# Thirteen more tiles of a two-block transformer are transposed on VectorE in 32 by 32 blocks

## Chip, core and metric

One core of a Trainium2 chip runs the whole program. The metric is the device time of one execution in microseconds, and of several executions the median. A profile is one further execution, recorded by the hardware profiler.

## What is computed

The reference takes 256 tokens of width 2048 through two transformer blocks, in float32. The first block has three mixers side by side (gated linear attention GLA, forgetting attention FoX, attention over a memory), a gated output projection and a feed-forward network. The second has an NSA attention with compressed, selected and window keys, a pooling mixer, a cross attention and a gated feed-forward network. Cut to what matters here:

```python
xn = rms_norm(h, attn_norm_g)
proj = xn @ w_in                      # gq gk gv gg ga fq fk fv fg ff mq mg
gla_o = gla_chunked(gq, gk, gv, log_a)
fq_h, fk_h = rms_norm(fq, fox_q_norm_g), rms_norm(fk, fox_k_norm_g)
fox_o = forgetting_attention(fq_h, fk_h, fv, log_f)
mk = rms_norm(mk, mem_k_norm_g); mq_h = rms_norm(mq, mem_q_norm_g)
mem_o = softmax(mq_h @ mk.T * 128 ** -0.5) @ mv
o = rms_norm(concat(gla_o, fox_o, mem_o), out_norm_g)
h = h + (o * gate) @ w_out
u = relu(rms_norm(h, mlp_norm_g) @ w_up)
h = h + (u * u) @ w_down
# second block: z = rms_norm(h, ...) @ w_in_2, a = nsa_attention(...), ... a @ w_br_attn
```

## The kernel before

**Weights and groups.** Each product with a weight matrix is a list of groups, one for each 512 output columns. A group has two PSUM banks, one for each half of 128 tokens, and takes 16 k-tiles of 128 rows. The product is made in three passes of fp32r numbers: a matrix is split into a high part (`wh`, a copy on ScalarE, line 133) and a low part (`wl`, a subtraction on VectorE, line 367), and so is the stationary operand (H and L). For each k-tile and each half there are three matmuls, H wh (line 461), H wl (462) and L wh (463). So a group is 96 matmuls of 512 columns. A unit is two k-tiles, 512 KB of weights, split in one instruction on each of the two engines. There are five raw buffers, filled from SyncE's queue, and six pairs wh, wl; a unit is split about four units ahead of its use (`AHEAD`).

**Order.** All engines' orders are written by a planner while the program is built. It walks through the groups in a fixed list (mk mv, then gq gk sm gv0 gv1 mq fq fk fv gg0 gg1 fg mg, out0 to out3, the feed-forward groups, then those of block 2). After every k-tile it calls `pump`, which first emits due weight splits and then lets tasks take a step each, as long as ScalarE and VectorE are by its own costs no more than `LIM` = 3500 ns behind TensorE. Tasks are generators: what is done with a finished group (its eviction, norms, transposes) and the attentions. A task that starts when another one has set an event (`until`) goes by the instruction having been emitted.

**Transposes.** H must have the model dimension on its partitions, so a result of 256 tokens by 512 columns, a tile of 128 x 1024 numbers, is transposed. `T_group` does it on TensorE: eight transposes of 128 x 128 (line 203) in two groups of four, each group into one of four PSUM banks `pb`, from which ScalarE and VectorE take the result, with a gain or split into H and L (`T_split`, `T_plain`). `T_dve` does it on VectorE, into another SBUF tile: 16 instructions of 32 partitions x 256 numbers (line 526), each of which transposes eight blocks of 32 x 32 and puts them in their places through its access pattern; then ScalarE copies H and VectorE subtracts to L. Before the change `T_dve` serves the tiles u of the first feed-forward network and those of the second, 27 in all.

**Who reads the tiles.** mkT, mqT, fqT and fkT are read by the score matmuls of memory attention and FoX (small matmuls, line 197); gqT and gkT by multiplications on VectorE in GLA, which feed small matmuls; the gated outputs by out0 to out3, four k-tiles each in the order of the tiles; the normed tiles h by up0 and all later up groups, in the same way; the two NSA outputs by four groups late in block 2.

Of the kernel before, what the change touches and what calls it, by code (L numbers as in the profile page):

```python
# [10 lines left out]
F32 = mybir.dt.float32  # L11
# [3 lines left out]
OP = mybir.AluOpType  # L15
# [93 lines left out]
class Program:  # L109
# [406 lines left out]

        yield from self.T_group(nat, sink)

    def T_dve(self, f, hi, lo):

        (g,) = yield from self.F.wait()
        x = f.rearrange("p (t k q j) -> p k t q j", t=2, k=4, q=4)
        y = g.rearrange("p (k t a i) -> p k t a i", k=4, t=2, a=4)
        for a in range(4):
            for q in range(4):
                self.nc.vector.transpose(y[32 * q:32 * q + 32, :, :, a], x[32 * a:32 * a + 32, :, :, q])  # L526
                self.dv(256)
                if q % 2:
                    yield 1
        self.F.put(f)  # L530
        self.act(hi, g)
        yield 1
        self.tt(lo, g, hi.bitcast(F32), OP.subtract)
        self.F.put(g)

    def T_plain(self, nat, dst, gain=None):
# [69 lines left out]
def v3(f, a):  # L606
    return f.rearrange("p (a b) -> p a b", a=a)


class Kernel(Program):  # L610
# [57 lines left out]
    def headnorm_T(self, banks, key, gain, name):  # L668
        yield from self.until(("rs", key))
        rs = self.rs[key]  # L670
        f, j = yield from self.F.wait(2)
        for t in range(2):
            self.scopy(v3(f, 2)[:, t], banks[t], rs[:, t:t + 1])
        yield "B"
        self.act(j, f, AF.Square)
        yield 1
        ss = self.stat(8)
        self.red(ss, v3(j, 8), OP.add)
        self.F.put(j)
        r = self.rstd(ss, 8, 128.0)  # L680
        yield 1
        self.tt(v3(f, 8), v3(f, 8), r[:, :, None].to_broadcast([128, 8, 128]), OP.mult)
        yield 1
        (o,) = yield from self.F.wait()
        yield from self.T_plain(v3(f, 2), o, gain)
        self.F.put(f)
        self.S[name] = o
        self.ev.add(name)

    def plain_T(self, banks, key, scale, name, keep=False):  # L690
        yield from self.until(("rs", key))
        rs = self.rs[key]
        if scale != 1.0:
            r2 = self.stat(2)
            self.ts(r2, rs, scale)
            rs = r2
        f, o = yield from self.F.wait(2)
        for t in range(2):
            self.scopy(v3(f, 2)[:, t], banks[t], rs[:, t:t + 1])
        yield "B"  # L700
        yield from self.T_plain(v3(f, 2), o)
        if keep:
            self.S["nat", name] = f
        else:
            self.F.put(f)
        self.S[name] = o
        self.ev.add(name)
# [316 lines left out]
    def gate(self, banks, grp, silu):  # L1024
        rs = self.rs["x"]
        (s,) = yield from self.F.wait()
        s3 = v3(s, 2)
        for t in range(2):
            self.act(s3[:, t], banks[t], AF.Sigmoid, scale=rs[:, t:t + 1])
            if silu:  # L1030
                self.stt(s3[:, t], banks[t], rs[:, t:t + 1], s3[:, t], OP.mult, OP.mult)
        if grp == 3:
            self.free_TT("x")
        yield "B"
        yield from self.until(("o", grp))
        o = self.S.pop(("o", grp))
        self.tt(o, o, s, OP.mult)
        self.F.put(s)
        yield 1
        h, l = yield from self.R.wait(2)  # L1040
        yield from self.T_split(v3(o, 2), self.vec("out_norm_g", 4 * grp, 4), h, l)
        self.F.put(o)
        self.TT["o"][0][grp], self.TT["o"][1][grp] = h, l
        self.ev.add(("oT", grp))

# [4 lines left out]
    def norm_T(self, f, c, key, gain, sq):  # L1050

        f3 = v3(f, 2)
        self.sq_into(f3, sq, c)
        self.nsq[key] = self.nsq.get(key, 0) + 1
        if self.nsq[key] == 4:
            self.fin_ssq(sq, key)
        yield 1
        h, l = yield from self.R.wait(2)
        yield from self.T_split(f3, self.vec(gain, 4 * c, 4), h, l)
        H, L = self.TT.setdefault(key, ([None] * 4, [None] * 4))  # L1060
        H[c], L[c] = h, l
        self.ev.add((key, c))
# [392 lines left out]

    def a_T(self, f, x):
        h, l = yield from self.R.wait(2)
        yield from self.T_split(v3(f, 2), None, h, l)
        self.F.put(f)
        self.TT["a"][0].append(h)  # L1460
        self.TT["a"][1].append(l)
        self.ev.add(("a", x))
# [697 lines left out]
```

## Time and profile before

| | us |
|---|---|
| median of 3 runs | 2615.86 (2615.46 to 2617.05) |
| the profiled execution, own time | 2612.74 |
| its span, first to last instruction | 2611.0 |
| TensorE busy | 2589.7 |
| VectorE busy | 1671.8 |
| ScalarE busy | 1265.4 |

TensorE was granted its full clock for 0.998 of the span. Matmuls are pipelined: the next one begins before the last one's record ends, so busy times of several lines of TensorE add up to more than the span, and the pace is read from the distance of starts. A wait is put down to what came last.

### The profile page before, as it was taken

The numbers are of one execution on the slowest core, as the hardware profiler recorded it, in microseconds if no ns is written. First come the engines' busy times: TensorE is split into PE (matmuls) and PEld (weight loads), VectorE is DVE, ScalarE is ACT, GpSimd is POOL, SyncE is SP. The second block draws the span as 40 slices with busy tenths as digits, with TensorE's granted clock in tenths as the row PEclk, the third lists the DMA queues.
The fourth block names the chain that finished last, engine by engine and source line by source line (L and its number), as shares of the span: only waits on it lengthen the run. The fifth ranks groups of instructions, "written<-read, shape, count | busy, mean of one in ns | idle before, by whom it ended". The sixth has DMA issues, their size and how long they took to land.

```text
span 2611.0 us, 31980 instructions
## 1 busy us (share of the span) xinstructions
PE 2589.7 (99%) x11980; PEld 2148.6 (82%) x11980; DVE 1671.8 (64%) x2310; ACT 1265.4 (48%) x1697; POOL 76.6 (3%) x97
## 2 busy tenths in 40 slices
PE   9999999999999999999999999999999999999998
PEld 7888888888888888888888888888788888888886
DVE  6567655686677567765566545666766656565656
ACT  7544544544444444454465444465554444444443
POOL 0001000000000000001000000000000000000001
PEclk9999999999999999999999999999999999999999
DMA  9543465555566556565444557655455556555653
GB/s 347 206 138 121 157 222 186 185 193 196 193 203 228 194 193 234 189 216 194 152 139 152 187 178 258 214 194 186 137 191 189 198 188 200 187 199 188 215 188 129
DMA packets 138893, 500.19 MB, mean 192 GB/s; under 512 B 15650, under 2 KB 16594, under 8 KB 138737
## 3 DMA queue, kind: packets, MB, share of 16 engines
q1 hardware_dynamic: 131760, 473.16, 53.5%
q0 software_dynamic: 6976, 24.98, 2.8%
q8 instruction: 94, 1.54, 0.2%
q14 instruction: 63, 0.51, 0.1%
HBM read 493.33 MB, written 7.88 MB: 192 GB/s over the span
## 4 chain that ended last, share of the span: by engine, by line
PE 94%; issue 4%; DVE 1%; DMA 0%; ACT 0%; POOL 0%; SPq 0%; DVEq 0%; ACTq 0%; POOLq 0%
PE gb L461 29%; PE gb L463 29%; PE gb L462 29%; PE pb L197 4%; PE pb L203 2%; DVE s L169 0%; DVE wl L367 0%; DMA s<-memT 0%; DVE s L158 0%; POOL st L233 0%; PE gb L451 0%; PE gb L453 0%; PE gb L452 0%; ACT s L133 0%; ACT wh L133 0%
## 5 line engine op out<-in xcount | busy, mean ns | idle before, releaser
L367 DVE TENSOR_TENSOR wl<-raw,wh 128x1024 fp32r<-128x1024 f32 (+1 forms) x876 | 1058.7, 1220 | 579.3 <-ACT wh L133 572.8
L461 PE MATMUL gb<-wh,s 128*128 128x512 f32 x3496 | 1380.4, 395 | 1.3 <-ACT wh L133 1.1
L462 PE MATMUL gb<-wl,s 128*128 128x512 f32 x3496 | 1363.4, 390 | 1.0 <-DVE wl L367 1.0
L463 PE MATMUL gb<-wh,s 128*128 128x512 f32 x3496 | 1364.3, 390 | 0.0
L133 ACT ACTIVATE wh<-raw 128x1024 fp32r<-128x1024 f32 (+1 forms) x878 | 917.3, 1055 | 820.4 <-PE gb L463 782.6
L461 PEld LDWEIGHTS gb<-wh,s 128*128 128x128 f32 x3496 | 657.5, 188 | 137.6 <-issue 3.1
L463 PEld LDWEIGHTS gb<-wh,s 128*128 128x128 f32 x3496 | 656.6, 188 | 138.4 <-DVE s L169 0.7
L462 PEld LDWEIGHTS gb<-wl,s 128*128 128x128 f32 x3496 | 657.6, 188 | 133.6 <-DVE wl L367 1.6
L526 DVE STREAM_TRANSPOSE s<-s 32x256 f32<-32x256 f32 x432 | 188.2, 436 | 7.8
L158 DVE TENSOR_TENSOR s<-gb,s 128x512 f32<-128x512 f32 x144 | 97.7, 690 | 111.0 <-PE gb L463 91.5
L133 ACT ACTIVATE s<-gb,st 128x512 f32<-128x512 f32 (+1 forms) x112 | 70.0, 642 | 177.8 <-PE gb L463 166.2
L133 ACT ACTIVATE s<-s 128x1024 fp32r<-128x1024 f32 (+3 forms) x89 | 82.5, 928 | 90.0 <-DVE s L526 68.5
L197 PE MATMUL pb<-s,s 128*128 128x128 f32 (+4 forms) x720 | 116.5, 301 | 1.3 <-DVE s L158 0.9
L197 PEld LDWEIGHTS pb<-s,s 128*128 128x128 f32 x720 | 97.7, 191 | 9.5 <-DVE s L158 1.3
L133 ACT ACTIVATE s<-pb 128x512 f32<-128x512 f32 (+4 forms) x117 | 56.9, 506 | 73.9 <-PE pb L203 49.7
L203 PE MATMUL pb<-cc,s 128*128 128x128 f32 (+1 forms) x484 | 73.6, 275 | 5.3 <-DVE s L169 5.3
L203 PEld LDWEIGHTS pb<-cc,s 128*128 128x128 f32 (+1 forms) x484 | 60.0, 141 | 22.1 <-DVE s L169 6.6
L158 DVE TENSOR_TENSOR s<-s,s 128x60 f32<-128x60 f32 (+5 forms) x123 | 73.8, 632 | 0.6
L133 ACT ACTIVATE s<-pb,vecs 128x256 fp32r<-128x256 f32 (+2 forms) x109 | 42.3, 453 | 51.3 <-PE pb L203 41.8
L163 DVE TENSOR_SCALAR s<-gb,st 128x512 f32<-128x512 f32 (+1 forms) x32 | 20.9, 659 | 67.8 <-PE gb L463 51.5
L169 DVE SCALAR_TENSOR_TENSOR s<-pb,vecs,s 128x256 fp32r<-128x256 f32 (+1 forms) x104 | 40.0, 435 | 29.9 <-ACT s L133 29.9
L133 ACT ACTIVATE s<-s,st 128x128 f32<-128x128 f32 (+2 forms) x73 | 32.8, 450 | 31.7 <-DVE st L163 30.4
(113 smaller groups left out, 551.1 us busy)
## 6 DMA issues: line engine op xcount, KB each, us to landing
raw<-w_in SPq DMA_DIRECT2D x216, 512.0 KB, 4.2
raw<-w_up SPq DMA_DIRECT2D x216, 512.0 KB, 4.4
raw<-w_down SPq DMA_DIRECT2D x216, 512.0 KB, 4.5
raw<-w_gate SPq DMA_DIRECT2D x88, 512.0 KB, 4.7
raw<-w_out SPq DMA_DIRECT2D x32, 512.0 KB, 4.6
raw<-w_mix_out SPq DMA_DIRECT2D x32, 512.0 KB, 4.7
raw<-w_br_pool SPq DMA_DIRECT2D x16, 512.0 KB, 5.2
raw<-w_br_attn SPq DMA_DIRECT2D x16, 512.0 KB, 4.4
```

The costliest lines, as they stand in the source:

```text
L133: self.nc.scalar.activation(out, in_, func, **kw)
L158: self.nc.vector.tensor_tensor(out, a, b, op)
L163: self.nc.vector.tensor_scalar(out, a, s1, None, op0=op0)
L169: self.nc.vector.scalar_tensor_tensor(out, a, s, b, op0, op1)
L197: self.nc.tensor.matmul(out, lhsT, rhs, start=start, stop=stop)
L203: self.nc.tensor.transpose(out, in_, self.ident[:k, :k])
L367: self.nc.vector.tensor_sub(l[:, :m], r, h[:, :m].bitcast(F32))
L461: mm(o, H[:, c:c + 128], wh, start=st, stop=False)
L462: mm(o, H[:, c:c + 128], wl, start=False, stop=False)
L463: mm(o, L[:, c:c + 128], wh, start=False, stop=sp)
L526: self.nc.vector.transpose(y[32 * q:32 * q + 32, :, :, a], x[32 * a:32 * a + 32, :, :, q])
```

## The change

`T_dve` is cut in two: `T_blocks` holds the 16 block transposes, and `T_dve` can now take a gain and leave the source tile in place. Thirteen tiles then use these in place of TensorE: mkT, mqT, fqT and fkT (the gain becomes one product in place over 128 x 1024), gqT and gkT (`keep` is set for these two alone), the gated outputs 0 to 2 of four, the normed tiles h 0 to 2 of four, and the first of two NSA outputs.

```diff
-    def T_dve(self, f, hi, lo):
-
-        (g,) = yield from self.F.wait()
+    def T_blocks(self, f, g):
+
         x = f.rearrange("p (t k q j) -> p k t q j", t=2, k=4, q=4)
         y = g.rearrange("p (k t a i) -> p k t a i", k=4, t=2, a=4)
         for a in range(4):
...
                 self.dv(256)
                 if q % 2:
                     yield 1
-        self.F.put(f)
-        self.act(hi, g)
-        yield 1
-        self.tt(lo, g, hi.bitcast(F32), OP.subtract)
+
+    def T_dve(self, f, hi, lo, gain=None, keep=False):
+
+        (g,) = yield from self.F.wait()
+        yield from self.T_blocks(f, g)
+        if not keep:
+            self.F.put(f)
+        if gain is None:
+            self.act(hi, g)
+            yield 1
+            self.tt(lo, g, hi.bitcast(F32), OP.subtract)
+        else:
+            self.split_T(v3(g, 4), gain, v3(hi, 4), v3(lo, 4))
+            yield 1
         self.F.put(g)
...
-        yield from self.T_plain(v3(f, 2), o, gain)
+        yield from self.T_blocks(f, o)
         self.F.put(f)
+        self.scopy(o, o, gain)
...
-        yield from self.T_plain(v3(f, 2), o)
+        if keep:
+            yield from self.T_blocks(f, o)
+        else:
+            yield from self.T_plain(v3(f, 2), o)
...
-        yield from self.T_split(v3(o, 2), self.vec("out_norm_g", 4 * grp, 4), h, l)
-        self.F.put(o)
+        if grp < 3:
+            yield from self.T_dve(o, h, l, self.vec("out_norm_g", 4 * grp, 4))
+        else:
+            yield from self.T_split(v3(o, 2), self.vec("out_norm_g", 4 * grp, 4), h, l)
+            self.F.put(o)
...
-        yield from self.T_split(f3, self.vec(gain, 4 * c, 4), h, l)
+        if key == "h" and c < 3:
+            yield from self.T_dve(f, h, l, self.vec(gain, 4 * c, 4), True)
+        else:
+            yield from self.T_split(f3, self.vec(gain, 4 * c, 4), h, l)
...
-        yield from self.T_split(v3(f, 2), None, h, l)
-        self.F.put(f)
+        if x == 0:
+            yield from self.T_dve(f, h, l)
+        else:
+            yield from self.T_split(v3(f, 2), None, h, l)
+            self.F.put(f)
```

How this moves instructions shows at two places. The first is the memory query mq in the GLA stretch (its tile before the transpose is `s_62`, transposed `s_68`; `s_38` is mkT; `s_64`, `s_65`, `s_71` and `s_72` are GLA's). TensorE before, around the first group of mq's transposes:

```order
L463 MATMUL gb_83<-wh_72,s_27_420 128x512
L203 MATMUL pb_87<-cc,s_62_1403 128x128 x4
L197 MATMUL pb_88<-s_42_686,s_49_1038 128x512
L197 MATMUL pb_88<-s_42_686,s_50_1039 128x512
L461 MATMUL gb_82<-wh_74,s_26_419 128x512
```

TensorE now, where the transposed tile is read for the first time:

```order
L197 MATMUL pb_87<-s_72_1557,s_65_1428 128x128 x4
L461 MATMUL gb_84<-wh_74,s_23_378 128x512
L462 MATMUL gb_84<-wl_75,s_23_378 128x512
L463 MATMUL gb_84<-wh_74,s_24_379 128x512
L461 MATMUL gb_85<-wh_74,s_23_378 128x512
L462 MATMUL gb_85<-wl_75,s_23_378 128x512
L463 MATMUL gb_85<-wh_74,s_24_379 128x512
L197 MATMUL pb_88<-s_38_634,s_68_1499 128x256 x2
```

The transposes are gone from TensorE's queue, and the reader stands behind GLA's own small matmuls. VectorE before, at the same tile:

```order
L158 TENSOR_TENSOR s_62_1403<-s_62_1403,st 128x1024
L367 TENSOR_TENSOR wl_71<-raw_66,wh_70 128x1024
L163 TENSOR_SCALAR s_68_1480<-pb_89,vecs 128x512
L367 TENSOR_TENSOR wl_73<-raw_67,wh_72 128x1024
L158 TENSOR_TENSOR s_64_1408<-s_64_1408,s_44_811 128x2x128
```

VectorE now:

```order
L158 TENSOR_TENSOR s_62_1422<-s_62_1422,st 128x1024
L525 STREAM_TRANSPOSE s_68_1499<-s_62_1422 32x8x32 x2
L367 TENSOR_TENSOR wl_71<-raw_66,wh_70 128x1024
L525 STREAM_TRANSPOSE s_68_1499<-s_62_1422 32x8x32 x4
L367 TENSOR_TENSOR wl_73<-raw_67,wh_72 128x1024
L525 STREAM_TRANSPOSE s_68_1499<-s_62_1422 32x8x32 x4
L158 TENSOR_TENSOR s_64_1427<-s_64_1427,s_44_824 128x2x128
...
L367 TENSOR_TENSOR wl_81<-raw_66,wh_80 128x1024
L525 STREAM_TRANSPOSE s_68_1499<-s_62_1422 32x8x32 x2
L173 TENSOR_REDUCE st<-s_74_1627 128x8
L165 TENSOR_SCALAR st<-st 128x8
```

The sixteen block transposes come in twos and fours between the low halves of the weights, the last two behind six of these and GLA's first level products. The second place is the normed tile h 2, made from group out2. VectorE before:

```order
L158 TENSOR_TENSOR s_103_2693<-gb_85,s_103_2693 128x512
L367 TENSOR_TENSOR wl_81<-raw_68,wh_80 128x1024
L367 TENSOR_TENSOR wl_71<-raw_69,wh_70 128x1024
L169 SCALAR_TENSOR_TENSOR s_112_3149<-pb_87,vecs,s_111_3148 128x256 x2
L367 TENSOR_TENSOR wl_73<-raw_65,wh_72 128x1024
L169 SCALAR_TENSOR_TENSOR s_112_3149<-pb_89,vecs,s_111_3148 128x256 x2
```

VectorE now:

```order
L158 TENSOR_TENSOR s_106_2752<-gb_85,s_106_2752 128x512
L367 TENSOR_TENSOR wl_81<-raw_68,wh_80 128x1024
L367 TENSOR_TENSOR wl_71<-raw_69,wh_70 128x1024
L525 STREAM_TRANSPOSE s_118_3235<-s_106_2752 32x8x32 x2
L367 TENSOR_TENSOR wl_73<-raw_65,wh_72 128x1024
L525 STREAM_TRANSPOSE s_118_3235<-s_106_2752 32x8x32 x4
...
L525 STREAM_TRANSPOSE s_118_3235<-s_106_2752 32x8x32 x4
L367 TENSOR_TENSOR wl_81<-raw_69,wh_80 128x1024
L169 SCALAR_TENSOR_TENSOR s_117_3234<-s_118_3235,vecs,s_116_3233 128x256 x4
L367 TENSOR_TENSOR wl_71<-raw_65,wh_70 128x1024
L158 TENSOR_TENSOR s_107_2754<-gb_82,s_107_2754 128x512
```

The four gain products that make L now follow the last block transposes, five low halves later than before and still ahead of the next group's adds.

## Rows read from the trace of the kernel before

**Rows 1.** The page's head: span, and busy time, share and instructions of each engine.

```profile
span 2611.0 us, 31980 instructions
PE 2589.7 (99%) x11980; PEld 2148.6 (82%) x11980; DVE 1671.8 (64%) x2310; ACT 1265.4 (48%) x1697; POOL 76.6 (3%) x97
```

**Rows 2.** TensorE's groups by form: busy us, mean ns, idle before.

```profile
L461 PE MATMUL gb<-wh,s 128*128 128x512 f32 x3496 | 1380.4, 395 | 1.3 <-ACT wh L133 1.1
L463 PE MATMUL gb<-wh,s 128*128 128x512 f32 x3496 | 1364.3, 390 | 0.0
...
L203 PE MATMUL pb<-cc,s 128*128 128x128 f32 x480 | 72.8, 275 | 5.3 <-DVE s L169 5.3
```

**Rows 3.** Timeline of TensorE around one group of four transposes: start us, us.

```profile
318.29 0.39 PE L463 MATMUL gb<-wh,s 128*128 128x512 f32 x1
318.52 0.60 PE L203 MATMUL pb<-cc,s 128*128 128x128 f32 x4
318.87 0.48 PE L461 MATMUL gb<-wh,s 128*128 128x512 f32 x1
...
320.12 0.39 PE L463 MATMUL gb<-wh,s 128*128 128x512 f32 x1
```

**Rows 4.** Stretches: length, busy us of each engine, clock, DMA share, GB/s.

```profile
160.00:275.00 115.00, 115.00 (x626) 98.52 (x625) 86.94 (x135) 51.70 (x81) 15.26 (x9) 1.00 0.40 135
...
520.00:600.00 80.00, 80.00 (x354) 66.30 (x354) 64.91 (x88) 38.71 (x40) 0.00 (x0) 1.00 0.60 199
600.00:1130.00 530.00, 530.00 (x2338) 438.32 (x2337) 364.33 (x450) 241.45 (x243) 8.52 (x15) 1.00 0.60 203
65.00:110.00 45.00, 45.00 (x236) 37.22 (x235) 26.00 (x26) 23.77 (x34) 4.91 (x7) 1.00 0.63 218
```

**Rows 5.** All waits of TensorE: us in total, times, longest us.

```profile
PE pb L203 <- DVE s L169: 5.3, 2, 4.4
PE pb L2041 <- DVE wh L2038: 2.0, 1, 2.0
PE gb L461 <- ACT wh L133: 1.1, 1, 1.1
PE gb L462 <- DVE wl L367: 1.0, 2, 0.8
PE pb L197 <- DVE s L158: 0.9, 1, 0.9
PE pb L197 <- DVE s L163: 0.3, 1, 0.3
```

**Rows 6.** The page's group of block transposes on VectorE.

```profile
L526 DVE STREAM_TRANSPOSE s<-s 32x256 f32<-32x256 f32 x432 | 188.2, 436 | 7.8
```

**Rows 7.** Timeline of VectorE, one tile u, its first and last rows.

```profile
499.58 0.87 DVE L526 STREAM_TRANSPOSE s<-s 32x256 f32<-32x256 f32 x2
500.48 1.23 DVE L367 TENSOR_TENSOR wl<-raw,wh 128x1024 fp32r<-128x1024 f32 x1
501.74 1.78 DVE L526 STREAM_TRANSPOSE s<-s 32x256 f32<-32x256 f32 x4
...
513.03 1.22 DVE L158 TENSOR_TENSOR s<-s,s 128x1024 fp32r<-128x1024 f32 x1
```

**Rows 8.** Timeline of VectorE, the residual adds of groups out2 and out3.

```profile
448.79 1.37 DVE L158 TENSOR_TENSOR s<-gb,s 128x512 f32<-128x512 f32 x2 [2.44 <-PE gb L463]
...
471.49 1.37 DVE L158 TENSOR_TENSOR s<-gb,s 128x512 f32<-128x512 f32 x2 [2.44 <-PE gb L463]
```

**Rows 9.** ScalarE's groups by form, products over a whole tile.

```profile
L133 ACT ACTIVATE s<-s 128x1024 f32<-128x1024 f32 x34 | 35.8, 1053 | 15.3 <-DVE s L169 9.0 <-DVE s L158 6.2
```

**Rows 10.** Timeline of VectorE, the second eviction of mqT.

```profile
202.74 0.75 DVE L163 TENSOR_SCALAR s<-pb,vecs 128x512 f32<-128x512 f32 x1 [1.24 <-PE pb L203]
```

**Rows 11.** Timeline of TensorE, memory attention's first scores.

```profile
206.20 1.02 PE L197 MATMUL pb<-s,s 128*128 128x256 f32 x4
```

**Rows 12.** Timeline of TensorE, a small matmul of attention that waits.

```profile
134.23 0.51 PE L197 MATMUL pb<-s,s 128*128 128x512 f32 x1 [0.95 <-DVE s L158]
```

## The prediction

> **What bounds the kernel now.** I read the page first: span, busy time by engine, clock. TensorE is busy in 2589.7 of 2611.0 us, VectorE in 1671.8, ScalarE in 1265.4 [rows 1]. A busy TensorE isn't yet a bound, since its rows overlap: the three multiplying lines of the weights have a mean of 390 to 395 ns [rows 2], but in the long feed-forward stretch 2338 matmuls fill 530.00 us [rows 4], one per 0.227 us. So I go by starts, not by durations. Next the waits of TensorE: over the whole run they add up to some 10.6 us, of which 5.3 us are transposes waiting for VectorE late in block 2, which the change doesn't touch, and 1.0 us is for the low halves of weights that VectorE makes [rows 5]. Everything else is TensorE following its own queue, at full clock. Hence the rule of this case: a matmul taken out gives back its pitch, and VectorE work put in costs nothing until TensorE waits for it.
>
> **What is removed.** Thirteen tiles of 128 x 1024 (mkT, mqT, fqT, fkT; gqT, gkT; three of the four gated outputs; three of the four normed tiles h; one of two NSA outputs) no longer pass TensorE. Each is eight transposes in two groups of four, so 104 transposes in 26 groups; the order of the program has 480 such transposes before and 376 after, and no other matmul goes or comes. What is a group worth? The row's mean is 275 ns [rows 2], which is a length in a pipeline and no price. In the timeline the group of four begins at 318.52 and the next weight matmul at 318.87, but the pipeline fills again behind it: from the weight matmul at 318.29 to the sixth one after it, at 320.12, are 1.83 us [rows 3], and six at 0.227 would be 1.36. The group costs 0.47 us by two-decimal starts. The other lone groups read between 0.45 and 0.47, and I take 0.46. 26 x 0.46 = **12.0 us** off TensorE.
>
> **What is added.** 13 x 16 = 208 block transposes at 436 ns [rows 6], 90.7 us on VectorE. The trace has 432 of them, 16 for each of 27 tiles, so duration and form are the kernel's own. VectorE goes from 1671.8 to some 1760 us of about 2600, from 64% to 68%. None of this counts by itself; what counts is whom TensorE waits for, place by place.
>
> *Low halves of the weights.* Queued behind the new transposes on VectorE is always the next low half (1.22 us). The planner makes it about four units of weights ahead, and a unit is twelve matmuls, 2.7 us: some 11 us of lead. The nearest evidence is the first feed-forward stretch, 520 to 600 us: 48 block transposes, VectorE busy 64.91 of 80 us, TensorE busy 80.00 of 80 [rows 4]. There one tile takes from 499.58 to the end of its subtraction at 514.25, 14.7 us, transposes and low halves taking turns [rows 7]. Cost nothing, as long as VectorE isn't more than some 8 us behind; from there each us is lost.
>
> *Normed tiles h, gated outputs, NSA output.* These are read by weight matmuls whose place is known. The tightest is h 2: its residual is added at 448.79; the adds at 471.49 show the next group ended there, so that up 0 starts, and it reaches h 2 at its ninth k-tile, 8 x 6 x 0.227 = 10.9 us later, at 482.4 [rows 8]. A tile took 14.7 us; with four gain products of some 0.5 us on each of two engines it is ready by about 470. Slack 12 us; h 0 and h 1 have one and two groups of 21.8 us (96 x 0.227) more. Gated outputs 0 to 2 stand in the same way to out 0. The fourth tiles, with a group less of time, stay on TensorE. The NSA output has twelve groups of weights before its reader. Cost nothing.
>
> *Keys and queries.* gqT and gkT feed VectorE products, in order behind the transposes. mkT is used 100 us later. fqT, fkT and mqT are read by small matmuls of attention, and there TensorE, in order, can be stopped. In the new program 25 weight matmuls, 5.7 us, stand between fkT's last instruction (the gain on ScalarE) and its first reader; for mqT only six weight matmuls and four small ones do, some 2.3 us. In this span VectorE must finish the last pair (0.9 us) and perhaps a low half (1.2 us), and ScalarE the gain in place (1.05 us for 128x1024 [rows 9], where two evictions stood before). Before, the eviction at 202.74 ended 2.7 us ahead of the reader at 206.20 [rows 10, 11]. I expect 0 to 2 us here.
>
> *VectorE in the GLA stretch.* From 160 to 275 us it is already 86.94 of 115.00 us busy while TensorE is busy 115.00 [rows 4]. Three tiles (mq, fq, fk) come in: 48 x 0.436 = 20.9 us, 107.9 in all, and six groups less shorten the stretch by 2.8 to 112.2: 96% busy. The trace shows nothing above 81% over such a stretch. So I bound it. From below: nothing, since TensorE had no idle there to win back (elsewhere in attention it once waited 0.95 us for VectorE [rows 12], which might go, so −1). From above: all 20.9 us, if each us of VectorE's idle was already needed for waits on the other engines. I take 1.5 us in all, mqT included: the nearest row is that single wait of about 1 us in the same kind of work, the planner holds tasks back while it counts VectorE as behind, and every us that TensorE does wait lets VectorE catch up.
>
> The sum: 2612.7 (the profiled execution's own time, 1.7 over its span) − 12.0 + 1.5 = 2602.2. The three runs' median, 2615.86, lies 3.1 us above that execution; I carry this over: 2615.86 − 10.5 = **2605.4 us**.
>
> **Rivals.** *A, slower: VectorE becomes the bound in the GLA stretch.* Small matmuls of GLA, FoX and memory attention then stand at the head of TensorE's queue waiting for products that are behind transposes. For it: 96%, and each GLA level is a chain VectorE to TensorE to VectorE. Against it: the weights' lead, and the new order spreads the tiles. If all 20.9 us land on the path, 2615.86 − 12.0 + 20.9 = 2624.8. It turns the sign once waits pass 12.0 us, 57% of what is added there. *A', the same in part*: 4 to 12 us lost, 2608 to 2616; middle 2612. The Trainium skill, "VectorE: DVE Perf Modes", section "Rules for kernel authors", is on this side: it tells authors to do 128 x 128 transposes on TensorE where PSUM will do as destination, and to keep VectorE for 32 x 32 ones. The trace agrees on the price, 7.0 us of VectorE a tile against 0.92 of TensorE; whether this decides depends on who has time to spare.
>
> *B, the removed transposes were worth their row's mean*: 104 x 275 ns = 28.6 us, and with 1.5 lost 2588.8. Against it are the starts, 0.35 us for four. The Trainium skill, "TensorE: Matmul & The Clock Gate", section "Part 4: PE-mode transpose", gives about 275 ns for one in a kernel (for bf16); by that price the sum would be this one. The trace has the same duration, and a pitch of about 0.11 us.
>
> *C, the early tiles' gain runs into the weights' DMA.* The keys mk and the GLA query and key save 6 x 0.46 = 2.8 us between 65 and 110 us, where DMA engines are still 0.63 busy [rows 4], after a start that was filled by loads. If weights bound there, these 2.8 us become a wait: 2608.2. Against it: in this stretch TensorE doesn't wait for weights, and later the DMA share is 0.6 or less.
>
> **Chances.** Forecast 0.73 (own range 2602.5 to 2608); A' 0.14; A beyond that 0.04; B 0.02; C 0.07. The likeliest case's middle is the prediction. The low end is the full 12.0 us plus the one wait that may go and 0.4 of scatter; the high end takes in C and half of A', to 2611.5, which leaves out less than 2 in 10. About 0.2%, 5.2 us, is what a measurement of this kernel tells from no change. Faster by more: forecast, B, C and half of A', 0.88. Within: the other half of A' and part of A, 0.09. Slower: 0.03.
>
> **What would show it.** In the new profile: 376 transposes on the TensorE line with unchanged pitch; VectorE at 68%, with 640 block transposes still near 436 ns; in the long feed-forward stretch nothing changed. TensorE's list of waits should grow by no more than about 2 us, at memory attention's first scores and in the GLA levels. Rival A would show there as VectorE above 95% and waits of small matmuls for it; a wait for low halves of weights would say that the lead was overrated. Rival B would show as a span near 2584, C as waits of ScalarE's weight copies for DMA before 110 us. The prediction is wrong if TensorE's waits between 160 and 300 us exceed 5 us, or if a group's price isn't 0.46.

## The result: 0.5% faster, 11.4 to 14.4 microseconds in four comparisons

In the first comparison the changed kernel takes 2601.29 us (median of 4 runs, 2600.78 to 2603.85) where the kernel before takes 2615.66 (4 runs, 2615.20 to 2617.05): ratio 0.9949, 95% interval 0.9938 to 0.9961. That is 14.4 us, where 10.5 were forecast and 2602.5 was the low end of the range; the direction was right, and the time lies 1.2 us under the range. Three more comparisons (below) give 11.8, 11.8 and 11.4 us. Over all of them, 81 runs of before have a median of 2615.06 and 19 of after 2602.55.

The profiled execution of after has its own time of 2603.85 us, the slowest of its four. The head of its page answers to [rows 1], with the two groups that the change touches, which answer to [rows 2] and [rows 6]:

```profile
span 2602.1 us, 31975 instructions
PE 2580.2 (99%) x11876; PEld 2138.5 (82%) x11876; DVE 1754.1 (67%) x2510; ACT 1269.7 (49%) x1697; POOL 79.6 (3%) x99
...
L203 PE MATMUL pb<-cc,s 128*128 128x128 f32 x376 | 57.7, 277 | 5.3 <-DVE s L169 5.3
...
L525 DVE STREAM_TRANSPOSE s<-s 32x256 f32<-32x256 f32 x640 | 278.8, 436 | 11.5
```

104 transposes have left TensorE and 208 block transposes have come to VectorE, each as long as the ones that were there. What decides is TensorE's list of waits. All of it (releaser, us in total, times, longest):

```profile
PE pb L203 <- DVE s L169: 5.3, 2, 4.4
PE pb L2063 <- DVE wh L2060: 2.0, 1, 2.0
PE gb L461 <- ACT wh L133: 1.6, 2, 1.1
PE gb L462 <- DVE wl L367: 1.0, 2, 0.8
PE pb L197 <- DVE s L158: 0.9, 1, 0.9
PE pb L197 <- DVE s L163: 0.3, 1, 0.3
```

Beside [rows 5] no line is new (2063 is the line that was 2041), and only the wait for `wh` has grown, by 0.5 us at the program's start. VectorE's 82 us more (90.7 of block transposes, less the evictions from `pb` that it no longer makes) have made TensorE wait nowhere in this execution. In one of three later profiles of the same kernel they have, for 0.70 us, in GLA's first level; the section on the prediction shows it.

**Where the time went.** Both programs issue the same 10,656 weight matmuls in the same order, so their count is a ruler: the nth one's start is compared in the two traces, and a stretch between two counts holds the same work but for what the change took out. One tile h shows it best, 48 weight matmuls with nothing else in the way. Before (start us, us):

```profile
426.57 0.39 PE L461 MATMUL gb<-wh,s 128*128 128x512 f32 x1
...
430.66 0.60 PE L203 MATMUL pb<-cc,s 128*128 128x128 f32 x4
...
432.49 0.60 PE L203 MATMUL pb<-cc,s 128*128 128x128 f32 x4
...
438.39 0.39 PE L461 MATMUL gb<-wh,s 128*128 128x512 f32 x1
```

After, the same two weight matmuls:

```profile
419.29 0.39 PE L461 MATMUL gb<-wh,s 128*128 128x512 f32 x1
...
430.17 0.39 PE L461 MATMUL gb<-wh,s 128*128 128x512 f32 x1
```

11.82 us have become 10.88: two groups of four, 0.47 us each. All stretches that differ, worked out in this way:

| weight matmuls | what lies there | before us | after us | difference | groups removed |
|---|---|---|---|---|---|
| 0 to 100 | start | 26.06 | 28.37 | +2.31 | 0 |
| 100 to 440 | mk, gq, gk | 74.94 | 72.20 | −2.74 | 6 |
| 740 to 1392 | mq, fq, fk, gated outputs | 185.91 | 180.43 | −5.48 | 12 |
| 1392 to 1776 | normed tiles h | 90.80 | 87.98 | −2.82 | 6 |
| 5480 to 5780 | first NSA output | 104.09 | 103.14 | −0.95 | 2 |
| 7400 to 7620 | late in block 2, untouched | 60.31 | 61.38 | +1.06 | 0 |

Every other stretch agrees within 0.02 us. The change itself gives −12.0 us; two stretches that it doesn't touch gave 3.4 back in this pair of executions. The three later profiles of after have the same −12.0 in the four stretches with groups removed; one of them loses 0.73 of it again between 440 and 740, where the 0.70 us of wait lie. So why 14.4 in the comparison? The runs without a profile had to say.

### The profile page after: what moved, and what is told of

It is laid out like the page before. It is cut to its first block, busy times and chain, and to the rows that moved or that the text cites. A ratio compares the mean times of both kernels' runs of the same rounds, so it can differ in the third digit from the quotient of the medians.

```text
span 2602.1 us, 31975 instructions
## 1 busy us (share of the span) xinstructions
PE 2580.2 (99%) x11876; PEld 2138.5 (82%) x11876; DVE 1754.1 (67%) x2510; ACT 1269.7 (49%) x1697; POOL 79.6 (3%) x99
## 4 chain that ended last, share of the span: by engine, by line
PE 94%; issue 4%; DVE 1%; DMA 0%; ACT 0%; POOL 0%; SPq 0%; DVEq 0%; ACTq 0%; POOLq 0%
PE gb L461 30%; PE gb L463 29%; PE gb L462 29%; PE pb L197 4%; PE pb L203 1%; DVE s L169 0%; DVE wl L367 0%; DMA s<-memT 0%; DVE s L158 0%; POOL st L233 0%; PE gb L451 0%; PE gb L452 0%; PE gb L453 0%; ACT s L133 0%; ACT wh L133 0%
## 5 line engine op out<-in xcount | busy, mean ns | idle before, releaser
L525 DVE STREAM_TRANSPOSE s<-s 32x256 f32<-32x256 f32 x640 | 278.8, 436 | 11.5
L203 PE MATMUL pb<-cc,s 128*128 128x128 f32 (+1 forms) x380 | 58.5, 277 | 5.3 <-DVE s L169 5.3
L203 PEld LDWEIGHTS pb<-cc,s 128*128 128x128 f32 (+1 forms) x380 | 47.7, 143 | 19.2 <-DVE s L169 6.6
L233 POOL TENSOR_TENSOR st<-st,nhalf 128x8 f32<-128x8 f32 (+2 forms) x21 | 28.0, 1331 | 674.4 <-DVE st L165 674.4
L133 ACT ACTIVATE s<-pb,vecs 128x256 fp32r<-128x256 f32 (+1 forms) x80 | 29.0, 434 | 33.3 <-PE pb L203 23.8
```

The costliest lines, as they stand in the source:

```text
L133: self.nc.scalar.activation(out, in_, func, **kw)
L203: self.nc.tensor.transpose(out, in_, self.ident[:k, :k])
L233: self.nc.gpsimd.tensor_tensor(r, t, self.nhalf[:, :k], op=OP.pow)
```

## Experiments

**1. Both kernels again, on other chips.** No edit. The theory, called 'clock' at first and 'scatter' later, says that the change is worth 12.0 us, and that the rest lies in the two untouched stretches, which differ from run to run. Against it stand 'more than transposes', by which the change gives something beyond the transposes, and 'profiler', by which a timed execution is always some 3 us longer than a profiled one.

> The kernel before once more, to see its spread. Theory 'clock': the kernel's work takes the same time each execution, and what differs is how many half-clock stretches of TensorE (3.4 us each, some 1.7 us lost in each) fall beside its waits near 15 us and 1880 us; the timed executions at 2615 to 2617 had two or three, the profiled one at 2612.74 had one. So times between 2611 and 2617 in steps of about 1.7, the slower ones with the lower mean clock. Rival 'profiler': a timed execution is always about 3 us longer than a profiled one; then no execution without an extra cause falls below 2615 and clock does not go with time.

> The changed kernel once more. Theory 'clock': with no half-clock stretch its execution would take 2598.9, each stretch adds 1.7; times between 2599 and 2605, and at equal mean clock 12.0 us below the kernel before. Rival 'more than transposes': a further 2.4 us is saved in each execution, so the difference at equal clock is 14.4.

> The changed kernel a third time, beside the kernel before on the same chip. The first comparison gave 14.4 us, the second 11.8. Theory 'scatter': the change is worth 12.0 us in every execution, and start and clock scatter each kernel by 4 us, so medians differ by 12 give or take 1.5. Rival 'more than transposes': 14.4 again.

> The changed kernel again, beside the kernel with three more tiles, on one chip: 2602.5 to 2603.5 against 2614.5 to 2616 before, 12 us apart.

Measured: before again 2615.20 (11 runs) against 2614.84 (27 runs), ratio 1.0002 (0.9993 to 1.0011). After 2603.01 against 2614.84, ratio 0.9951 (0.9938 to 0.9965); 2602.51 against 2614.28 (21 runs), 0.9954 (0.9941 to 0.9966); 2603.06 against 2614.48 (9 runs), 0.9955 (0.9941 to 0.9969). Differences 11.8, 11.8, 11.4: 'scatter' holds. Each interval alone still has room for 14.4, but the fifteen repeats together don't: with 14.4 half of them would lie under 2600.66 (2615.06 less 14.4), and none does; the lowest is 2600.67. So 'more than transposes' falls. Single runs of before go from 2612.66 to 2617.19, so the profiled execution of 2612.74, which lay 3.1 us under the three runs' median, was nearly the fastest of all, and 'profiler' falls too. Slower runs have the lower mean clock, as 'clock' said: of 77 runs of before the 24 at 0.998 have a median of 2613.9, the 50 at 0.997 one of 2615.4. Steps of 1.7 us, which it also expected, aren't to be seen in these times.

Where most of the scatter sits, the clock column shows. Two windows of before, two of after, one of before's second profile (stretch: length, busy us of each engine with instructions, granted clock, DMA share, GB/s):

```profile
15.70:19.10 3.40, 3.40 (x16) 2.81 (x15) 3.40 (x7) 3.26 (x7) 0.00 (x0) 1.00 1.03 409
1883.80:1887.20 3.40, 3.40 (x12) 2.57 (x11) 3.40 (x8) 2.17 (x8) 0.87 (x1) 0.50 0.44 180
```

```profile
15.70:19.10 3.40, 3.40 (x8) 2.68 (x9) 3.40 (x6) 3.40 (x6) 0.00 (x0) 0.50 1.02 411
1872.50:1879.30 6.80, 5.82 (x20) 4.73 (x21) 6.37 (x15) 2.43 (x9) 1.98 (x2) 0.50 0.42 161
```

```profile
1883.60:1890.40 6.80, 5.30 (x19) 4.30 (x19) 6.80 (x15) 2.18 (x8) 2.50 (x2) 0.50 0.52 190
```

Column clock: 0.50 is 1.2 GHz, 1.00 is 2.4. At the start, after's TensorE makes 8 matmuls in 3.4 us where before's makes 16. Late in block 2, before spends 3.4 us at half clock in one profile and 6.8 in the other: the same program. Over the 13 profiles of this study the first 100 weight matmuls take 26.06 to 28.98 us and the late stretch 59.90 to 61.48; together 4.5 us, as wide as the runs of before. Late in block 2 the clock divides them: 59.90 to 60.49 in the six with 3.4 us at half clock, 60.79 to 61.48 in the seven with 6.8. At the start it does so too (26.06 to 27.63 in the six without half clock, 27.96 to 28.98 in the seven with it), but there 1.6 us differ at full clock, and why they do wasn't looked into.

**2. Six of the thirteen tiles alone.** mk, mq, fq, fk, gq and gk on VectorE, the gated outputs, the tiles h and the NSA output back on TensorE:

```diff
-        if grp < 3:
+        if grp < 0:
...
-        if key == "h" and c < 3:
+        if False:
...
-        if x == 0:
+        if x < 0:
```

> Only the six tiles of keys and queries (mkT, mqT, fqT, fkT, gqT, gkT) on VectorE, the gated outputs, h and the NSA output on TensorE as before. Theory 'pitch': 12 of 26 groups, 5.5 us below the kernel before, 2609.3, no new wait although VectorE is as full in the GLA stretch as in the changed kernel. Rival 'chains are shorter': the transposes on TensorE cost more there than their pitch, since they sit in front of attention's small matmuls, 8 us or more below, 2606.5.

Measured: 2609.31 (10 runs) against 2614.28, ratio 0.9979 (0.9970 to 0.9988), 5.0 us. On the ruler −0.36, −2.38, −5.45 and +2.76 in a row of stretches (the mixers' order is another one, so work moves between the last two), in all −5.4 for 12 groups: 0.45 each. No wait of TensorE is new. So 'pitch' holds and 'chains are shorter', which expected 8 us or more, falls: the price is one of the group and not of the place, and the half of the change that was thought risky, attention's keys and queries, gives its full share.

**3. Twice the block transposes in the GLA stretch.** mqT, fqT and fkT are transposed a second time into the same tile (the result is the same; 48 block transposes, 20.9 us, do nothing):

```diff
         yield from self.T_blocks(f, o)
+        if key == "x":
+            yield from self.T_blocks(f, o)
```

> The changed kernel with the 16 block transposes of mq, fq and fk done twice (the second time over the first), 48 more on VectorE, 20.9 us, in the GLA stretch, nothing else changed. Theory 'cover': VectorE still finishes ahead of TensorE's needs because the planner spreads the tiles; TensorE waits grow by 0 to 3 us, time 2601 to 2604. Rival 'saturation': VectorE is at 96% there already, so most of the 20.9 us land on TensorE, 2610 to 2622.

Measured: 2615.52 (10 runs) against 2614.84, ratio 1.0003 (0.9994 to 1.0012): 12.5 us over after in the same comparison, the whole gain. 'Cover' falls, and the time is in the range of 'saturation'. But the loss isn't where that theory and the prediction looked for it. TensorE's longest wait, and its timeline at that place:

```profile
PE gb L461 <- ACT s L133: 9.9, 1, 9.9
```

```profile
387.25 0.39 PE L463 MATMUL gb<-wh,s 128*128 128x512 f32 x1
397.54 0.80 PE L461 MATMUL gb<-wh,s 128*128 128x512 f32 x1 [9.90 <-ACT s L133]
398.13 0.63 PE L462 MATMUL gb<-wl,s 128*128 128x512 f32 x1
398.56 0.63 PE L463 MATMUL gb<-wh,s 128*128 128x512 f32 x1
```

VectorE up to then, and the window's clock:

```profile
388.63 1.22 DVE L367 TENSOR_TENSOR wl<-raw,wh 128x1024 fp32r<-128x1024 f32 x1
389.77 7.17 DVE L525 STREAM_TRANSPOSE s<-s 32x256 f32<-32x256 f32 x16
397.52 1.68 DVE L169 SCALAR_TENSOR_TENSOR s<-s,vecs,s 128x256 fp32r<-128x256 f32 x4 [0.57 <-ACT s L133]
```

```profile
391.10:401.30 10.20, 3.77 (x9) 3.01 (x10) 8.58 (x18) 2.65 (x5) 0.00 (x0) 0.50 0.15 49
```

The waiting matmul is out 0's first one on the third gated output, the last tile of its kind on VectorE. Its sixteen block transposes begin at 389.77, after TensorE is already waiting. And the wait has a tail: the clock stands at half until 401.3, and the matmuls start 0.43 us apart instead of 0.23. 9.9 us of wait and 1.9 of half clock (3.8 us from 397.54 on) are 11.8; on the ruler that stretch is 11.9 longer than in after. GLA itself has one short wait of 0.57 us, at the same place as the 0.70 us of after's later profile.

Why so late, 100 us behind GLA? In the GLA stretch VectorE is hardly fuller than in after (102.01 us of 160 to 275 against 101.51). The ruler shows that attention's steps moved on: weight matmuls 740 to 1110 take 13.7 us less than in after, 1110 to 1392 14.6 more, and from 275 us to the end of the wait VectorE is busy 111.41 of 122.40 us, where after has 92.53 of 111.00 up to 386 us. The planner's code holds tasks back when VectorE is behind by its own costs; that this is what moved them is the likely reading, not tested by itself. The bill is paid where weight matmuls need the last product of that chain. In after this tile is ready 8.4 us ahead of its reader. Whether a planner with another limit would hide these 20.9 us wasn't tried.

**4. The fourth gated output and the fourth tile h too.** They are read with a group less of time:

```diff
-        if grp < 3:
+        if grp < 4:
...
-        if key == "h" and c < 3:
+        if key == "h":
```

> The changed kernel with the fourth gated output and the fourth normed tile h on VectorE too. Two tiles less on TensorE save 4 x 0.46 = 1.8 us. Theory 'slack': these have about 8 us from the end of the eviction to the reader, and a tile takes some 10 us longer on VectorE than on TensorE, so TensorE waits 2 to 5 us at out 0 and again at up 0; time 2603 to 2609, and waits of L461 or L463 for VectorE or ScalarE tiles appear. Rival 'hidden': no wait appears, time 2599.5.

Measured: 2611.09 (10 runs) against 2614.84, ratio 0.9984 (0.9975 to 0.9993): 8.1 us over after in the same comparison, a little more than 'slack' had in its range. 'Hidden' falls. There are two waits for the fourth tiles, 6.1 us in all; the longer one on TensorE, then VectorE and ScalarE ahead of it:

```profile
397.38 0.79 PE L461 MATMUL gb<-wh,s 128*128 128x512 f32 x1 [4.53 <-ACT s L133]
397.97 0.63 PE L462 MATMUL gb<-wl,s 128*128 128x512 f32 x1
```

```profile
393.73 1.23 DVE L367 TENSOR_TENSOR wl<-raw,wh 128x1024 fp32r<-128x1024 f32 x1
394.99 1.79 DVE L525 STREAM_TRANSPOSE s<-s 32x256 f32<-32x256 f32 x4
```

```profile
396.81 1.70 ACT L133 ACTIVATE s<-s,vecs 128x256 fp32r<-128x256 f32 x4 [5.58 <-DVE s L525]
```

The last four block transposes end at 396.78, the gain follows at once, and out 0 starts on it at 397.38. The clock is at half from 396.6 to 403.4, which adds some 3 us. 4.53 and 1.54 (at up 0) of wait, 3 of clock, less 1.8 for four groups removed: 7.3, against 7.7 on the ruler. These two tiles rightly stay on TensorE. Another 2.9 us of this profile lie long before the fourth tiles, in GLA's first level, where TensorE waits 1.20 us and then works at half clock from 133.8 to 137.2.

**5. More tiles of block 2.** The second NSA output, and the first two of four tiles h2 and y, which stand in rows of groups of only 48 matmuls:

```diff
-        if key == "h" and c < 3:
+        if (key == "h" and c < 3) or (key == "h2" and c < 2):
...
-        if x == 0:
-            yield from self.T_dve(f, h, l)
-        else:
-            yield from self.T_split(v3(f, 2), None, h, l)
-            self.F.put(f)
+        yield from self.T_dve(f, h, l)
...
-        yield from self.T_split(v3(y, 2), None, h, l)
-        self.F.put(y)
+        if c < 2:
+            yield from self.T_dve(y, h, l)
+        else:
+            yield from self.T_split(v3(y, 2), None, h, l)
+            self.F.put(y)
```

> The changed kernel with five more tiles on VectorE: the second NSA output, the first two of the four normed tiles h2 (the stream that enters block 2) and the first two of the four tiles y before the mixer's output. The trace of the changed kernel has 28 and 22 us between the TensorE version of h2 0 and 1 and their reader, 27 and 21 for y 0 and 1, 194 for the NSA output, and a tile takes some 10 us longer on VectorE. Theory 'pitch and slack': ten groups of 0.46 us less and no new wait, so 4.6 us below the changed kernel, 2598. Rival 'late stalls': VectorE's evictions and residual adds at the end of the first block stand behind the transposes, a wait of some us at h2 or y, 2601 to 2606.

Measured: 2615.94 (11 runs) against 2614.28, ratio 1.0004 (0.9995 to 1.0013): 13.4 over after in the same comparison. 'Pitch and slack' falls; 'late stalls' named the right kind of loss and put it far too low. New waits:

```profile
PE gb L461 <- ACT s L133: 8.2, 2, 6.8
...
PE gb L463 <- DVE s L158: 4.1, 2, 2.0
```

VectorE where the tiles y are made, then TensorE's two reads of them:

```profile
1666.02 2.36 DVE L367 TENSOR_TENSOR wl<-raw,wh 128x1024 fp32r<-128x1024 f32 x2
1668.29 0.68 DVE L158 TENSOR_TENSOR s<-pb,s 128x512 fp32r<-128x512 f32 x1
1668.99 0.89 DVE L525 STREAM_TRANSPOSE s<-s 32x256 f32<-32x256 f32 x2
1669.91 1.29 DVE L158 TENSOR_TENSOR s<-gb,s 128x512 f32<-128x512 f32 x2
1671.12 1.22 DVE L158 TENSOR_TENSOR s<-s,s 128x1024 fp32r<-128x1024 f32 x1
1672.25 1.22 DVE L367 TENSOR_TENSOR wl<-raw,wh 128x1024 fp32r<-128x1024 f32 x1
```

```profile
1672.38 0.51 PE L463 MATMUL gb<-wh,s 128*128 128x512 f32 x1 [2.02 <-DVE s L158]
...
1685.36 0.80 PE L461 MATMUL gb<-wh,s 128*128 128x512 f32 x1 [6.78 <-ACT s L133]
```

From 1651 to 1684 VectorE's rows stand end to end without one wait. The low part of y 0 (the subtraction at 1671.12) ends at 1672.34, and the matmul that waits for it starts at 1672.38; y 1's transposes end at 1684.2. On the ruler against after this row is 11.9 us longer, that of h2 2.3 (two waits, 1.40 and 0.38 us), and GLA's first level 2.3 (a wait of 0.69 us, then half clock from 135.5 to 138.9), while h2's two tiles and the NSA output gave back 0.94 each. A count of VectorE's work from its rows fits this: 48 matmuls last 10.9 us, in which VectorE owes four low halves (4.9 us), a residual's adds (1.3), a product over the tile or more (1.2 each), and now 7.0 of transposes and 1.2 of subtraction, over 15 in all. In a group of 96 it owes twice the low halves and the rest once, some 20 us of 21.8.

**6. One tile of each row, and the second NSA output alone.** The edits of experiment 5 with `c < 1` for h2 and for y; and only its middle part (the NSA output):

> Three more tiles on VectorE than in the changed kernel: the second NSA output, and of the tiles h2 and y of block 2 (four each, one per group of 48 matmuls, 10.9 us) only the first, where an earlier kernel moved two of each and gained nothing. Theory 'budget': in a stretch of groups of 48 matmuls VectorE has 10.9 us a group and needs about 8 before a tile is transposed there (4.9 low halves, 1.3 adds, 1.2 to 2 gain products), so one tile of 7 us eats the spare time of about two groups and a second one right behind it can't be paid. A single tile is paid back before the row of four ends: six groups of four transposes at 0.46 less, 2.8 us, under the changed kernel (about 2600 against 2602.8), and no wait for VectorE beyond the short ones that the changed kernel has. Rival 'no room at all': the evictions and adds of the next tiles queue behind the transposes of the first, and the matmuls that need their banks or their tiles wait, half as much as with two of each: 2604 to 2610.

> One more tile on VectorE than in the changed kernel: the second NSA output, whose groups stand in a stretch of block 2 where the first one gained 0.95 us in the comparison of the two traces. Both theories, 'budget' and 'no room at all', expect 0.9 us less than the changed kernel, about 2601.9, which a measurement can't tell from it; the trace is what counts: the stretch before its reader shorter by 0.9 us, no new wait. If waits appear here, the second NSA output and not h2 or y is where the kernel with two tiles of each lost a part of its time.

> The kernel with three more tiles again, beside the changed kernel on one chip. By the stretches of its trace it is worth 2.0 us more (three tiles at 0.94, less a wait of 0.8 for the residual add in the row of y tiles): 2 us under the changed kernel of this run, 14 under before. Rival: its lead of 1.2 to 2 us over the earlier runs of the changed kernel was scatter at the start, then it lies within 1 us of it.

Measured: with three more tiles 2600.84 against 2615.94 (9 runs), ratio 0.9942 (0.9930 to 0.9955), and 2601.42 against 2614.48, 0.9949 (0.9937 to 0.9962), there 1.6 us under after on the same chip. With the NSA output alone 2601.71 against 2615.94, 0.9946 (0.9932 to 0.9960). Times can't tell these from after (the intervals overlap), the ruler can: h2 −0.94, NSA output −0.94, y −0.94 and +0.83. The one new wait that both profiles of the kernel with three tiles have is y's:

```profile
1666.08 1.22 DVE L158 TENSOR_TENSOR s<-s,s 128x1024 fp32r<-128x1024 f32 x1
```

```profile
1667.35 0.50 PE L463 MATMUL gb<-wh,s 128*128 128x512 f32 x1 [0.54 <-DVE s L158]
```

'Budget' holds for h2 and the NSA output, and for y just so: a single tile in such a row is paid for, a second one behind it is not, but even the first y is late by half a microsecond at its low part, where 'budget' expected no wait. 'No room at all' falls. By its trace this kernel is 2.0 us under after, the best of the study, with y 0 adding only 0.1 of them.

## Why the prediction was right in direction and missed its range

**The price of a group, 0.46 us.** Right to within a hundredth: 26 groups, −12.0 us on the ruler, and 5.4 for 12 of them alone. Rival B, the row's mean as a price, is out: the row still says 277 ns for a transpose, and eight of them gave back 0.94 us. The Trainium skill, "TensorE: Matmul & The Clock Gate", section "Part 4: PE-mode transpose", gives about 275 ns for one in a kernel (for bf16). This trace, in fp32, has the same as a duration, and 0.46 us for four as a price.

**The added work, 1.5 us.** That it would cost next to nothing was right; the term of the sum was mis-sized. It measured 0.0 in three of four profiles of after and 0.7 in the fourth. The prediction looked for it at mqT, before memory attention's first scores. There after's ScalarE (the gain), then TensorE:

```profile
219.67 1.15 ACT L133 ACTIVATE s<-s,vecs 128x1024 f32<-128x1024 f32 x1 [1.27 <-DVE s L525]
...
221.54 1.02 PE L197 MATMUL pb<-s,s 128*128 128x256 f32 x4
```

The gain ends 0.7 us ahead of the reader, so the 0 to 2 us expected there came out at its lower end. For fkT it was 3.7 us.

The one wait lies earlier, at tiles that the prediction took as safe. The window 65 to 110 us of after, where mk, gq and gk are transposed, answers to [rows 4], where VectorE was busy 26.00 us:

```profile
65.00:110.00 45.00, 45.00 (x224) 36.99 (x223) 40.58 (x65) 24.43 (x36) 6.84 (x9) 1.00 0.63 226
```

That is 90%, and from 85 to 122 us it is 35.95 of 37.00, 97%, where before had 18.07, and far fuller than the stretch that was feared (below). GLA's first products stand behind these transposes on VectorE. In after's second profile, whose first 100 weight matmuls took 26.60 us instead of 28.37, ScalarE waits for them, and then TensorE waits for ScalarE:

```profile
125.39 1.06 ACT L133 ACTIVATE s<-s 128x1024 f32<-128x1024 f32 x1 [1.79 <-DVE s L169]
```

```profile
131.34 0.50 PE L197 MATMUL pb<-s,s 128*128 128x512 f32 x1 [0.70 <-ACT s L133]
```

In before, with 26.06 us for the same start, this matmul didn't wait. So the added work is nearly hidden, with no time left over at this place.

**The GLA stretch, 96%.** It didn't come to that. The window 160 to 275 us, which answers to [rows 4]:

```profile
160.00:275.00 115.00, 115.00 (x613) 98.24 (x612) 101.51 (x172) 52.00 (x79) 13.66 (x8) 1.00 0.39 138
```

VectorE has 14.6 us more, not 20.9, 88%: 42 of the 48 block transposes (18.3 us) fall into the window, the others behind it, and evictions and other rows of 3.7 us have left it, which the prediction had not taken off. TensorE waits nowhere between 160 and 300 us, so the sign of being wrong that was set there didn't come. Rival A didn't occur as it stood, but experiment 3 shows how near it was: as much again, and 12.5 us are gone. Its mechanism was misplaced: apart from 0.57 us it was not small matmuls waiting in GLA, but the gated output at out 0, which the prediction had counted among the safe ones. The Trainium skill, "VectorE: DVE Perf Modes", section "Rules for kernel authors", leaves 128 x 128 transposes to TensorE where PSUM will do as destination. Here TensorE is the bound, and for these thirteen tiles 7.0 us of VectorE each were cheaper than 0.92 of TensorE. Experiments 3 to 5 are on the rule's side: there VectorE has no time left before the reader.

**Normed tiles.** The slack of 12 us for h 2 was about right: its H part is ready 15.7 us ahead of its reader, with h 0 and h 1 at 47 and 31.

**Rival C** didn't occur: the early 2.74 us were kept up to weight matmul 440 in all four profiles of after, and in the first from 40 to 110 us ScalarE's weight copies wait 1.1 us for DMA, before 2.2.

**The step that failed** is the last one, where the level was carried over and the range was set. "The three runs' median, 2615.86, lies 3.1 us above that execution; I carry this over" took three runs as the level, 0.8 us too high: 81 have 2615.06. The term for the added work put on 1.5 us that weren't paid. And the range's low end, the full 12.0 us, a wait of 1 us and "0.4 of scatter", left no room for what single executions differ by, 4.5 us. With the median of many and no loss the sum is 2615.06 − 12.0 = 2603.1; the 19 runs of after have 2602.55, 0.5 lower, and the first four lay 1.3 under that, which was chance. So of the 4.1 us between 2605.4 and 2601.3, 2.3 are the prediction's own terms and 1.8 scatter that its range had no place for. The three-run interval of 1.6 us, set beside a profiled execution 2.7 us under its lowest run, was the sign to read: it showed scatter wider than the interval. One slip in the chances: forecast, B, C and half of A' add up to 0.89, not 0.88.

## What to carry to other kernels

Where one engine bounds, work taken from it is worth its pitch, and the best proof is a ruler of matched instructions: it gave the same 12.0 us in four profiles of after where run times scatter by 4.5. Work moved to another engine is free as long as that engine meets each reader, so count its time between two readers (a group of 96 matmuls had room for a tile, a group of 48 hardly), not its share of the span. Look at every stretch where the work lands (here 65 to 122 us was fuller than the one that was feared), look for the price downstream, at the last product of a delayed chain, and add the half clock that followed the long waits here.

## What was not expected of the hardware

- The same wait has two clocks behind it. Late in block 2 TensorE waits 4.40 us in before, 4.42 in before's second profile and 4.41 in after; half clock then lasts 3.4 us in the first and 6.8 in the other two. At the start the two longest waits agree within 0.02 us (1.10 and 0.75 before, 1.12 and 0.77 after; after has one more of 0.45 ahead of them), and only after had half clock behind them.
- Half clock came with each of the longest waits: from 3.5 us into the wait of 9.9 us until 3.8 us after its end; around the wait of 6.78 us (experiment 5) from 1681.7 to 1691.9; around that of 4.53 us (experiment 4) from 396.6 to 403.4. With short waits it differs: one of 1.54 us (experiment 4) had none; waits of 1.20 and 0.95 us, 1.45 us apart in GLA, were followed by it from 133.8 to 137.2 (experiment 4), and 0.69 and 0.95 us at the same place from 135.5 to 138.9 (experiment 5), but not 0.70 and 0.95 us in after's second profile.
- Where TensorE doesn't wait, its pace repeats to 0.03 us over hundreds of microseconds: 2,948 weight matmuls from 1900 to 4848 take 672.00 us in before and after.
